# Thirteen instead of eleven tile pairs of an up projection by seven products, eight of them without a full tile between every two

## The chip, the cores and the metric

One core of a Trainium2 chip runs the whole kernel. The metric is the device time of one execution in microseconds (us), the median of several. Below, PE is the matrix engine, DVE the vector engine, ACT the scalar engine, POOL the general one, and SP the queue that issues most loads. POOL issues the loads that add to what is in the buffer already.

## The reference, cut to what matters

A decoder layer for 512 tokens and 1024 channels: three token mixers, an output projection, and then a gated feed-forward part, which the change touches:

```python
h2 = rms_norm(x, norm_ffn[l])                                    # 512 x 1024
up = causal_dwconv(h2 @ w_up[l], ffn_conv_w[l], ffn_conv_b[l])   # w_up 1024 x 6144, width 3
gate_h, val_h = jnp.split(up, 2, axis=-1)                        # 3072 channels each
x = x + (jax.nn.gelu(gate_h, approximate=True) * val_h) @ w_down[l]
```

## The kernel before, in words

The output of the up projection is made in 24 pairs of tiles: pair `i` is 128 gate channels and the 128 value channels that belong to them, each for all 512 tokens. Every float32 factor is split into a high and a low part (`split`, L97 on ACT makes the high part, L98 on DVE the low one), and each product is three matmuls instead of one (`mm3`, L104: high by high, high by low, low by high).

**A full pair** is two units, one for the gate tile and one for the value tile. A unit loads 128x1024 weights into one of three `raw` buffers (L167), splits them into `whi` and `wlo`, and runs 8 x 3 = 24 matmuls with 512 columns. Its result goes through the convolution: one ACT pass (L1184) and two DVE passes, called taps here (L1186). Gate and value meet in a gelu (L1198, ACT) and a product (L1199, DVE).

**A pair by seven products** (`up_fast`) halves the 1024 input channels and the 512 tokens, and needs seven products of half size instead of eight. Each product is 4 x 3 = 12 matmuls with 256 columns, 84 in all. Its weights are blocks of w_up: B11 and B21 (upper and lower half of the input channels) of the gate tile, B12 and B22 of the value tile.

| product | weights | PSUM bank | what reads the bank |
|---|---|---|---|
| a1 | B11 | x | ACT copy (L1290) into the first half of the gate |
| a2 | B21 | its own | DVE addition (L1292) to that half |
| c1 | B11+B12 | c | ACT copy into the second half of the value |
| c2 | B22 | c, on top of c1 | ACT copy into the first half of the value |
| b1 | B11+B12+B22 | x, on top of a1 | DVE subtraction (L1295) from that half |
| b2 | B12+B22 | x, on top of b1 | DVE subtraction from the second half of the value |
| b3 | B11+B12+B22+B21 | x, on top of b2 | ACT copy into the second half of the gate, then taps, gelu, product |

Because a1, b1, b2 and b3 accumulate in one bank, each must have been read before the next begins. The sums of weights are made by POOL in the buffer: after a1's split has read B11, a load that adds brings B12 on top of it (L1273), after c1's split B22, after b1's split B21. So each pair has four plain loads of 256 KB on SP (L1264), four adding loads of 256 KB on POOL, and seven splits of 128x512.

The work is a list of units (a full tile or one product), and what prepares a unit is written so many units ahead:

```python
"a1": [(10, lambda: load("B11")), (5, lambda: ready("a1", "B11", "B12"))],
...
"b1": [(2, lambda: ready("b1", "B11", "B21"))],
"b2": [(10, lambda: load("B12")), (7, lambda: add("B12", "B22")), (1, lambda: ready("b2", "B12"))],
```

So a1's split is written five units ahead of a1, and the load that adds B12 stands behind it. A scheduler then moves instructions a little against each other. All buffers of 128x512 that are not weights of full tiles come from one pool of 51 slots; `whi` and `wlo` have four buffers each.

The order before: pairs 0, 1, 2 are full. Then each of eleven pairs by products is written over two periods, and each period holds one full unit D: `b1' a1 D b2' c1 a2 b3' c2` (the mark is for the pair before). Pairs 5, 8, 11, 14, 17 and 19 give these full units, pairs 20 to 23 follow with the down projection. A small subtraction for the down projection (`down_s3`, L1315, DVE) stands at the end of most periods.

Of the kernel before, what the change touches and what calls it, by code (L numbers as in the profile page):

```python
# [9 lines left out]
F32R = mybir.dt.float32r  # L10
# [8 lines left out]
P = 128  # L19
# [15 lines left out]
NF = FF // P  # L35
# [22 lines left out]
def trunk(ctx: ExitStack, tc: tile.TileContext, x, xT, mem, memT, par, wdecay, wch, wv, wg, wmk,  # L58
# [4 lines left out]
    wpool = pool("wpool", NWB)  # L63
# [8 lines left out]
    def nm(s):  # L72
        uid[0] += 1
        return f"{s}_{uid[0]}"
# [4 lines left out]
    def rslot(shape=(P, S)):  # L79
        return apool.tile(list(shape), F32R, tag="s", name=nm("r"))  # L80
# [121 lines left out]
    HB = D // 2  # L202
# [351 lines left out]
    def proj_in(i, evac):  # L554
        return wch[i], D, lambda w: evac(channel_major(w, KD, lambda k: (hh[:, k, :], hl[:, k, :])))
# [222 lines left out]
    b2 = [u for d in range(KD) for u in branch(2, oc, d)]  # L778
# [423 lines left out]
    def up_units(tiles, keep, early=0):  # L1202

        us = []
        first = []
        for n in range(2 * len(tiles)):
            i, half = tiles[n // 2], n % 2
            if n < early:

                def fn(w, n=n):  # L1210
                    first.append((w, channel_major(w, KD, h2k, 0, S // 2)))
                    if n != 1:
                        norm2_flip(2 + n // 2)
# [40 lines left out]
            return h2["h"][at], h2["l"][at]  # L1254
        return tuple(a[:, k % 2, :] for a in h2s[key, k // 2])

    def up_fast(i, keep):

        src = lambda q: wup[NF * (int(q[2]) - 1) + i][:, HB * (int(q[1]) - 1):HB * int(q[1])]
        raw, w, st = {}, {}, {}  # L1260

        def load(q):
            raw[q] = fslot()
            loads.append(nc.sync.dma_start(raw[q], src(q)))  # L1264

        def ready(key, q, more=None):
            w[key] = rslot(), rslot()
            split(*w[key], raw[q])
            if more:
                add(q, more)  # L1270

        def add(q, more):
            nc.gpsimd.dma_start(raw[q], src(more), accum_op=ALU.add)  # L1273

        def run(key):
            if key == "a1":
                st["x"], st["o"] = bank((P, HT)), (fslot(), fslot())
            elif key in ("a2", "c1"):
                st[key] = sbank((P, HT))
            ps = st["c1" if key[0] == "c" else "a2" if key == "a2" else "x"]  # L1280
            hi, lo = w.pop(key)
            k = range(KD // 2)
            mm3(ps, [(*(a[:, j * P:(j + 1) * P] for a in (hi, lo)), *h2_part(key, j)) for j in k],
                key in ("a1", "a2", "c1"), True, key not in ("a1", "a2", "c1"))
            (g, v), tt = st["o"], nc.vector.tensor_tensor

            one, two = slice(0, HT), slice(HT, S)
            if key in ("a1", "c1", "c2", "b3"):
                o = {"a1": g[:, one], "c1": v[:, two], "c2": v[:, one], "b3": g[:, two]}[key]
                nc.scalar.activation(o, ps, AF.Copy)  # L1290
            elif key == "a2":
                tt(out=g[:, one], in0=g[:, one], in1=ps, op=ALU.add)  # L1292
            else:
                o = v[:, one if key == "b1" else two]
                tt(out=o, in0=o, in1=ps, op=ALU.subtract)  # L1295
            if key == "b3":
                up_mix(*(up_evac(a, NF * half + i) for half, a in enumerate((g, v))), i, keep)

        pre = {
            "a1": [(10, lambda: load("B11")), (5, lambda: ready("a1", "B11", "B12"))],  # L1300
            "a2": [(7, lambda: load("B21")), (3, lambda: ready("a2", "B21"))],
            "c1": [(3, lambda: ready("c1", "B11", "B22"))],
            "c2": [(6, lambda: load("B22")), (3, lambda: ready("c2", "B22"))],
            "b1": [(2, lambda: ready("b1", "B11", "B21"))],
            "b2": [(10, lambda: load("B12")), (7, lambda: add("B12", "B22")), (1, lambda: ready("b2", "B12"))],
            "b3": [(2, lambda: ready("b3", "B11"))],
        }
        return {key: (p, lambda key=key: run(key)) for key, p in pre.items()}

# [107 lines left out]
    us = up_units((0, 1, 2), whole, 3)  # L1417
# [1 line left out]
        us[5], [lambda: h2_ready("c2", 0), lambda: h2_ready("c2", 1)])  # L1419


    us = up_units((5, 8, 11, 14, 17, 19), whole) + up_units(range(20, NF), whole)
    ahead = None
    for i, even in zip((3, 4, 6, 7, 9, 10, 12, 13, 15, 16, 18), (None, 0, 2, None, 4, 6, 8, 10, 12, 14, None)):
        f = up_fast(i, whole)
        run([ahead["b1"]] if ahead else [], [f["a1"]], us.pop(0))
        run([ahead["b2"]] if ahead else [], [f["c1"], f["a2"]], [ahead["b3"]] if ahead else [], [f["c2"]])
        if not ahead:
            run([lambda k=k, p=p: h2_ready(k, p) for k in ("b1", "b2") for p in range(2)])
        if even is not None:  # L1430
            run([lambda i=even: down_s3(i)])
        ahead = f
    run([ahead["b1"]], us.pop(0), [lambda: down_s3(16)], [ahead["b2"]], us.pop(0), [ahead["b3"]], [lambda: down_s3(18)])
    down, n = down_fast(5), 0
    for i, u in enumerate(us):
        run(u, down[5 * i:5 * i + 5 if u is not us[-1] else -4])
# [97 lines left out]
```

## Time and profile before

| what | value |
|---|---|
| median of 3 runs | 918.35 us (917.28 to 918.51) |
| profiled execution | 918.04 us, its span 916.3 us |
| PE busy in the span | 906.1 us (99%) |
| DVE, ACT, POOL busy | 661.6 us (72%), 536.4 us (59%), 145.4 us (16%) |
| full units and products, one after the other | 545 to 738 us of the span |
| mean clock granted to PE | 0.998 |

A row of the timeline or of the chain gives the start in the span, the length, the engine, the line, and how many equal instructions it merges ("x12"). The names say what is written from what: `mm<-h2h,whi` is a matmul of a full unit, `mm<-r,r` or `sm<-h2h,r` one of a product, `r<-f,r` the low part of a split, `wlo<-raw,whi` that of a full unit. In brackets stands how long the engine was idle before, and who ended that. A table by stretches gives the busy time of each engine, the granted clock, the share of time in which the DMA engines worked, and what they moved.

### The profile page before, as it was taken

Reading aid. Unit: us, or ns where it says so; the run is one execution under the profiler, and the core shown is the slowest. Engines: PE = TensorE matmul, PEld = TensorE weight load, DVE = VectorE, ACT = ScalarE, POOL = GpSimd, SP = SyncE. Lnnn points to the kernel's source line nnn. Section 1 sums busy time; section 2 is a strip of 40 time slices with the busy share of each in tenths; the row PEclk is TensorE's granted clock in tenths of the full one; section 3 lists DMA queues with packets and bytes.
Section 4 is the critical chain, followed back from the end, with each engine's and each line's share of the span. In section 5 each row is a group of like instructions: output and inputs, shape, how many; then the busy total and the mean of one; then the engine's idle time right before and its main releaser. Section 6 shows DMA issues by size and latency. Waiting matters only on the chain.

```text
span 916.3 us, 13261 instructions
## 1 busy us (share of the span) xinstructions
PE 906.1 (99%) x4786; PEld 789.1 (86%) x4786; DVE 661.6 (72%) x1194; ACT 536.4 (59%) x935; POOL 145.4 (16%) x188
## 2 busy tenths in 40 slices
PE   9999999999999999999999999999999999999996
PEld 7899888888889998888888898999999988888785
DVE  6996854665679568655867588768777679977665
ACT  7765654685865469475534356656565555555544
POOL 0010000000243330221000000122222221315102
PEclk9999999999999999999999999999999999999999
DMA  7446323213377784331147224776767686779612
GB/s 254 130 141 219 99 82 101 82 49 121 106 175 160 187 198 133 111 101 53 37 152 258 70 79 123 174 188 137 204 141 188 139 194 138 163 201 247 139 46 92
DMA packets 55505, 128.55 MB, mean 140 GB/s; under 512 B 6624, under 2 KB 14480, under 8 KB 55440
## 3 DMA queue, kind: packets, MB, share of 16 engines
q1 hardware_dynamic: 37088, 94.99, 31.5%
q0 software_dynamic: 18208, 32.46, 20.7%
q8 instruction: 37, 0.61, 0.3%
q10 hardware_dynamic: 144, 0.26, 0.1%
q14 instruction: 28, 0.23, 0.1%
HBM read 123.23 MB, written 3.67 MB: 138 GB/s over the span
## 4 chain that ended last, share of the span: by engine, by line
PE 89%; DMA 4%; DVE 3%; ACT 2%; issue 1%; POOL 0%; SPq 0%; POOLq 0%; DVEq 0%; ACTq 0%
PE mm L104 77%; PE sm L104 7%; DMA f<-in_wdown 2%; PE mm L443 2%; DMA f<-in_wv 1%; DVE wlo L98 1%; PE sm L1021 1%; DVE f L399 0%; PE sm L1007 0%; PE sm L1023 0%; DMA raw<-in_wch 0%; PE sm L994 0%; DVE f L565 0%; DVE r L98 0%; PE sm L1162 0%
## 5 line engine op out<-in xcount | busy, mean ns | idle before, releaser
L98 DVE TENSOR_TENSOR wlo<-raw,whi 128x1024 fp32r<-128x1024 f32 (+3 forms) x133 | 146.3, 1105 | 65.9 <-ACT whi L97 36.1
L97 ACT ACTIVATE whi<-raw 128x1024 fp32r<-128x1024 f32 (+3 forms) x133 | 125.6, 953 | 114.7 <-PE mm L104 83.3
L104 PE MATMUL mm<-whi,r 128*128 128x512 f32 (+2 forms) x568 | 168.6, 373 | 0.4 <-DVE r L98 0.4
L104 PEld LDWEIGHTS mm<-whi,r 128*128 128x128 f32 x568 | 105.5, 188 | 16.6 <-DVE r L98 0.8
L97 ACT ACTIVATE r<-f 128x512 fp32r<-128x512 f32 (+3 forms) x184 | 91.9, 542 | 41.1 <-DMA f<-in_wup 37.3
L104 PE MATMUL mm<-hh,whi 128*128 128x512 f32 x288 | 113.2, 393 | 0.0
L104 PE MATMUL mm<-hl,whi 128*128 128x512 f32 x288 | 112.4, 390 | 0.0
L104 PE MATMUL mm<-wlo,r 128*128 128x512 f32 (+2 forms) x284 | 105.7, 372 | 0.5 <-DVE wlo L98 0.5
L98 DVE TENSOR_TENSOR r<-f,r 128x512 fp32r<-128x512 f32 (+3 forms) x184 | 102.3, 586 | 4.0 <-ACT r L97 3.7
L104 PE MATMUL mm<-r,whi 128*128 128x512 f32 (+1 forms) x432 | 94.2, 367 | 0.0
L104 PEld LDWEIGHTS mm<-r,whi 128*128 128x128 f32 x432 | 75.2, 189 | 13.1
L1273 POOL DMA_DIRECT2D f<-in_wup x44 | 38.6, 983 | 283.1 <-DVE r L98 232.6
L104 PE MATMUL mm<-r,r 128*128 128x256 f32 (+2 forms) x456 | 81.6, 329 | 0.0
L97 ACT ACTIVATE whi<-f 128x512 fp32r<-128x512 f32 (+2 forms) x90 | 48.2, 579 | 55.7 <-PE mm L104 41.0
L104 PEld LDWEIGHTS mm<-r,r 128*128 128x128 f32 (+1 forms) x456 | 68.8, 187 | 9.7 <-ACT r L97 0.2
L98 DVE TENSOR_TENSOR wlo<-f,whi 128x512 fp32r<-128x512 f32 (+2 forms) x90 | 53.6, 632 | 31.0 <-ACT whi L97 28.1
L104 PE MATMUL mm<-h2l,whi 128*128 128x512 f32 (+1 forms) x200 | 75.7, 382 | 0.0
L104 PE MATMUL mm<-h2h,whi 128*128 128x512 f32 (+1 forms) x200 | 75.4, 382 | 0.0
L104 PE MATMUL mm<-hh,wlo 128*128 128x512 f32 x288 | 71.5, 390 | 0.0
L104 PEld LDWEIGHTS mm<-hh,wlo 128*128 128x128 f32 x288 | 54.0, 188 | 11.2
L104 PEld LDWEIGHTS mm<-hl,whi 128*128 128x128 f32 x288 | 54.1, 188 | 10.9
L104 PEld LDWEIGHTS mm<-hh,whi 128*128 128x128 f32 x288 | 54.1, 188 | 10.9
(258 smaller groups left out, 1613.6 us busy)
## 6 DMA issues: line engine op xcount, KB each, us to landing
raw<-in_wch SPq DMA_DIRECT2D x39, 512.0 KB, 3.5
raw<-in_wup SPq DMA_DIRECT2D x26, 512.0 KB, 4.4
f<-in_wup SPq DMA_DIRECT2D x44, 256.0 KB, 6.1
f<-in_wup POOLq DMA_DIRECT2D x44, 256.0 KB, 5.7
f<-in_wdown POOLq DMA_DIRECT2D x40, 256.0 KB, 8.2
raw<-in_wbr SPq DMA_DIRECT2D x24, 384.0 KB, 3.1
raw<-in_wdown SPq DMA_DIRECT2D x14, 512.0 KB, 5.1
f<-in_wdown SPq DMA_DIRECT2D x20, 256.0 KB, 5.6
```

The source lines that it names most:

```text
L97: nc.scalar.activation(hi, src, AF.Copy)
L98: return (eng or nc.vector).tensor_tensor(out=lo, in0=src, in1=hi.bitcast(F32), op=ALU.subtract)
L104: nc.tensor.matmul(ps, lhsT=l, rhs=r, start=first and i == 0, stop=last and i == len(seq) - 1, skip_group_check=more)
L443: nc.tensor.matmul(ps[u], lhsT=w(a, u, k), rhs=xs["r"][k][j], start=k == 0 and i < n, stop=k == KD - 1 and i >= len(seq) - n)
L1021: nc.tensor.matmul(ps[:, j, :], lhsT=sT[h][:, t, :], rhs=vt[t][hp][:, j, :], start=True, stop=t == 0)
L1273: nc.gpsimd.dma_start(raw[q], src(more), accum_op=ALU.add)
```

## The change

Pairs 3, 4, 6, 8 to 16 and 18 are now made by seven products (thirteen), and pairs 5, 7, 17, 19 and 20 to 23, beside 0 to 2, are full. The first eight of the thirteen are written over three periods each. One period is now `a1 c1' D? b1'' c2' b2'' a2 b3''`, where one mark is for the pair before and two marks are for the pair before that, and D, a full unit, stands only in four of the ten periods (counted from 0: in 1, 4, 7 and 8). The last five pairs have the order of before: the first of the five begins in period 9, beside the end of the eight and with a full unit between its a1 and its c1; the second has no full unit, and the other three have one each. a1 and b1 of the first eight are prepared earlier (six and five units ahead), b3 later (one unit ahead). The split weights of c1 and c2 move from the pool of 51 slots into the two halves of a `whi` and a `wlo` buffer.

```diff
-    def up_fast(i, keep):
+    def up_fast(i, keep, deep):
...
         def ready(key, q, more=None):
-            w[key] = rslot(), rslot()
+            if key == "c1":
+                st["w"] = [wpool.tile([P, 2, HB], F32R, tag=t, name=nm(t)) for t in ("whi", "wlo")]
+            w[key] = tuple(a[:, int(key[1]) - 1, :] for a in st["w"]) if key[0] == "c" else (rslot(), rslot())
             split(*w[key], raw[q])
...
         pre = {
-            "a1": [(10, lambda: load("B11")), (5, lambda: ready("a1", "B11", "B12"))],
+            "a1": [(11, lambda: load("B11")), (6, lambda: ready("a1", "B11", "B12"))] if deep else
+                  [(10, lambda: load("B11")), (5, lambda: ready("a1", "B11", "B12"))],
             "a2": [(7, lambda: load("B21")), (3, lambda: ready("a2", "B21"))],
             "c1": [(3, lambda: ready("c1", "B11", "B22"))],
             "c2": [(6, lambda: load("B22")), (3, lambda: ready("c2", "B22"))],
-            "b1": [(2, lambda: ready("b1", "B11", "B21"))],
+            "b1": [(5 if deep else 2, lambda: ready("b1", "B11", "B21"))],
             "b2": [(10, lambda: load("B12")), (7, lambda: add("B12", "B22")), (1, lambda: ready("b2", "B12"))],
-            "b3": [(2, lambda: ready("b3", "B11"))],
+            "b3": [(1 if deep else 2, lambda: ready("b3", "B11"))],
         }
...
-    us = up_units((5, 8, 11, 14, 17, 19), whole) + up_units(range(20, NF), whole)
-    ahead = None
-    for i, even in zip((3, 4, 6, 7, 9, 10, 12, 13, 15, 16, 18), (None, 0, 2, None, 4, 6, 8, 10, 12, 14, None)):
-        f = up_fast(i, whole)
-        run([ahead["b1"]] if ahead else [], [f["a1"]], us.pop(0))
-        run([ahead["b2"]] if ahead else [], [f["c1"], f["a2"]], [ahead["b3"]] if ahead else [], [f["c2"]])
...
+    us = up_units((5, 7, 17, 19), whole) + up_units(range(20, NF), whole)
+    nd = 8
+    fast = [up_fast(i, whole, k < nd) for k, i in enumerate((3, 4, 6, 8, 9, 10, 11, 12, 13, 14, 15, 16, 18))]
+    even = {1: 0, 2: 2, 4: 4, 5: 6, 6: 8, 8: 10, 10: 12, 11: 14}
+    part = lambda k, key: [fast[k][key]] if 0 <= k < nd else []
+    for k in range(nd + 2):
+        run(part(k, "a1"), part(k - 1, "c1"))
+        if k in (1, 4, 7, 8):
+            run(us.pop(0))
+        run(part(k - 2, "b1"), part(k - 1, "c2"), part(k - 2, "b2"), part(k, "a2"))
+        if k == nd + 1:
+            run([fast[nd]["a1"]], us.pop(0), [fast[nd]["c1"], fast[nd]["a2"]])
+        run(part(k - 2, "b3"))
...
+    run([fast[nd]["c2"]])
+    for k in range(nd + 1, len(fast)):
+        f, g = fast[k], fast[k - 1]
+        run([g["b1"], f["a1"]], us.pop(0) if k > nd + 1 else [], [g["b2"], f["c1"], f["a2"], g["b3"], f["c2"]])
...
```

On PE, 96 matmuls with 512 columns go and 168 with 256 columns come, over the whole program.

Three places of the order as built. **DVE between the subtraction that reads b1 and the one that reads b2.** Before (line 1295 reads the bank, `r` are splits of products, `wlo` that of a full unit, line 1186 are taps):

```order
L1295 TENSOR_TENSOR f_5997<-f_5997,mm_5995 128x256
L1199 TENSOR_TENSOR f_6125<-f_6125,f_6129 128x512
L98 TENSOR_TENSOR r_6170<-f_5951,r_6169 128x512
L1315 TENSOR_TENSOR f_6125<-f_6125 128x256
L98 TENSOR_TENSOR r_6195<-f_5993,r_6194 128x512
L98 TENSOR_TENSOR r_6199<-f_6110,r_6198 128x512
L98 TENSOR_TENSOR wlo_6885<-raw_6882,whi_6884 128x1024
L1186 SCALAR_TENSOR_TENSOR f_6227<-mm_6202,prm,f_6227 128x511
L1295 TENSOR_TENSOR f_5997<-f_5997,mm_5995 128x256
```

Now, in a period without a full unit (lines 1295 and 1315 have become 1297 and 1318; the rows begin with the taps that follow b3 of the pair before):

```order
L1186 SCALAR_TENSOR_TENSOR f_6110<-f_5653,prm,f_6110 128x510
L1186 SCALAR_TENSOR_TENSOR f_6114<-f_5654,prm,f_6114 128x510
L98 TENSOR_TENSOR r_6140<-f_6036,r_6139 128x512
L1199 TENSOR_TENSOR f_6110<-f_6110,f_6114 128x512
L98 TENSOR_TENSOR r_6161<-f_6081,r_6160 128x512
L1297 TENSOR_TENSOR f_5799<-f_5799,mm_5797 128x256
L98 TENSOR_TENSOR r_6178<-f_5982,r_6177 128x512
L1318 TENSOR_TENSOR f_6110<-f_6110 128x256
L98 TENSOR_TENSOR r_6197<-f_5710,r_6196 128x512
L98 TENSOR_TENSOR r_6218<-f_5544,r_6217 128x512
L1297 TENSOR_TENSOR f_5799<-f_5799,mm_5797 128x256
L98 TENSOR_TENSOR wlo_6357<-f_6036,whi_6356 128x512
```

The full unit's split and taps are gone from between the two subtractions, and what is there belongs to the next products: the split of b2 itself, of the next b1, and of b3.

**PE between b2 and b3 in such a period**, now (`mm_5945` is the shared bank; the first row ends b2, the last begins b3; `sm_6369` is a2, `mm_6415` the next pair's a1). Before, all 24 matmuls of c1 and a2 stood here:

```order
L104 MATMUL mm_5945<-r_5645,r_6323 128x256 x2
L104 MATMUL sm_6369<-h2h,r_6303 128x256
L104 MATMUL sm_6369<-h2l,r_6303 128x256
L104 MATMUL sm_6369<-h2h,r_6303 128x256
L104 MATMUL sm_6369<-h2l,r_6303 128x256
L104 MATMUL sm_6369<-h2h,r_6304 128x256 x4
L104 MATMUL mm_6415<-h2l,r_6284 128x256
L104 MATMUL mm_5945<-h2h,r_6352 128x256
```

Nine matmuls are left between b2 and b3; in the same period 23 stand between b1 and b2 (7 of a1, 12 of c2, 4 of a2).

**ACT around c1's split.** Before (line 1184 opens the convolution, `r_6351` is c1's split, whose buffer has just been added to, line 1198 the gelu, `whi_7066` a full unit):

```order
L1184 ACTIVATE f_6310<-f_5997,prm 128x512
L1290 ACTIVATE f_6180<-sm_6258 128x256
L97 ACTIVATE r_6351<-f_6135 128x512
L1198 ACTIVATE f_6306<-f_6306 128x512
L1290 ACTIVATE f_6361<-mm_6360 128x256
L97 ACTIVATE r_6376<-f_6176 128x512
L97 ACTIVATE r_6380<-f_6291 128x512
L97 ACTIVATE whi_7066<-raw_7064 128x1024
```

Now, for the second of the last five pairs, the one that has no full unit (`whi_6901<-f_6696` is c1's split, `r_6923` the split for b2 of the pair before):

```order
L1184 ACTIVATE f_6882<-f_6417,prm 128x512
L1292 ACTIVATE f_6773<-sm_6824 128x256
L97 ACTIVATE whi_6901<-f_6696 128x512
L97 ACTIVATE r_6923<-f_6726 128x512
L97 ACTIVATE whi_7047<-raw_7045 128x1024
L1198 ACTIVATE f_6878<-f_6878 128x512
L97 ACTIVATE whi_6901<-f_6906 128x512
```

The split of b2 and the gelu now stand behind c1's split, which reads a buffer that is being added to.

More of the change, by code (lines that the diff above doesn't have):

```diff
@@ L1419, in trunk @@
         us[5], [lambda: h2_ready("c2", 0), lambda: h2_ready("c2", 1)])
-    us = up_units((5, 8, 11, 14, 17, 19), whole) + up_units(range(20, NF), whole)
-    ahead = None
-    for i, even in zip((3, 4, 6, 7, 9, 10, 12, 13, 15, 16, 18), (None, 0, 2, None, 4, 6, 8, 10, 12, 14, None)):
-        f = up_fast(i, whole)
-        run([ahead["b1"]] if ahead else [], [f["a1"]], us.pop(0))
-        run([ahead["b2"]] if ahead else [], [f["c1"], f["a2"]], [ahead["b3"]] if ahead else [], [f["c2"]])
-        if not ahead:
-            run([lambda k=k, p=p: h2_ready(k, p) for k in ("b1", "b2") for p in range(2)])
[L1430 to L1433, printed above, removed]
+    us = up_units((5, 7, 17, 19), whole) + up_units(range(20, NF), whole)
[11 more added lines that the diff above has]
+        run(part(k - 2, "b3"))
+        if k == 1:
+            run([lambda k=k, p=p: h2_ready(k, p) for k in ("b1", "b2") for p in range(2)])
+        if k in even:
+            run([lambda i=even[k]: down_s3(i)])
+    run([fast[nd]["c2"]])
+    for k in range(nd + 1, len(fast)):
+        f, g = fast[k], fast[k - 1]
+        run([g["b1"], f["a1"]], us.pop(0) if k > nd + 1 else [], [g["b2"], f["c1"], f["a2"], g["b3"], f["c2"]])
+        if k in (10, 11):
+            run([lambda i=even[k]: down_s3(i)])
+    run([fast[-1]["b1"]], us.pop(0), [lambda: down_s3(16), fast[-1]["b2"], fast[-1]["b3"], lambda: down_s3(18)])
     down, n = down_fast(5), 0
```

## The prediction

> **What bounds the kernel now.** I read the page's totals first, then the chain of work that ended last, then a table by stretches, and then the timelines of the engines in one period.
>
> ```profile
> span 916.3 us, 13261 instructions
> PE 906.1 (99%) x4786; PEld 789.1 (86%) x4786; DVE 661.6 (72%) x1194; ACT 536.4 (59%) x935; POOL 145.4 (16%) x188
> ...
> PE 89%; DMA 4%; DVE 3%; ACT 2%; issue 1%; POOL 0%; SPq 0%; POOLq 0%; DVEq 0%; ACTq 0%
> ```
>
> PE works 99% of the span, and 89% of the chain that sets the end is PE. In the stage of the change nothing else is on it:
>
> ```profile
> 598.03 9.78 PE mm L104 x60
> 607.81 2.88 PE sm L104 x24
> 610.69 1.44 PE mm L104 x12
> 612.13 1.44 PE sm L104 x12
> ...
> core 0: us, PE busy (x) PEld busy (x) DVE busy (x) ACT busy (x) POOL busy (x), PEclk, DMA share, GB/s
> 582.00:598.00 16.00, 15.97 (x112) 14.80 (x111) 11.13 (x19) 10.15 (x20) 2.98 (x5) 1.00 0.86 232
> 644.65:660.19 15.54, 15.54 (x111) 14.58 (x110) 11.82 (x20) 8.94 (x17) 3.89 (x6) 1.00 0.70 162
> ```
>
> The chain's four rows are one period: b1, a1, D and b2 (60 matmuls), c1 and a2 (24), b3, c2. They follow each other without a gap, 15.54 us in all, and the last row of the table says the same of another period: PE 15.54 of 15.54 us at full clock. DVE is busy for 76% of it, the DMA engines for 70%. So here PE's own work sets the time, and the question is what it costs to bring more of it per microsecond to the helpers.
>
> **PE's work.** What a full unit and a product take is read from PE's timeline:
>
> ```profile
> 647.37 0.40 PE L104 MATMUL mm<-h2h,whi 128*128 128x512 f32 x1
> 652.84 1.59 PE L104 MATMUL mm<-r,r 128*128 128x256 f32 x12
> 658.59 1.60 PE L104 MATMUL sm<-r,r 128*128 128x256 f32 x12
> 672.21 0.64 PE L104 MATMUL sm<-h2h,r 128*128 128x256 f32 x4
> ```
>
> A full unit begins at 647.37 and the next product at 652.84: 5.47 us for 24 matmuls, 0.228 each. The chain's 24 matmuls of products take 2.88 us: 1.44 a product, 0.120 a matmul. A full pair is 2 x 5.47 = 10.94 us, a pair by products 7 x 1.44 = 10.08. Two pairs change sides: 4 x 5.47 = 21.88 us go, 20.16 come. PE saves **1.72 us**, and as PE never waited in this stage, no more than that can come from it.
>
> The Trainium skill (TensorE: Matmul & The Clock Gate, "Back-to-back issue gap") gives N/2.4 + 2.5 ns for an isolated matmul of N columns, 215.8 ns for 512 and 109.2 for 256. Estimated from that page, the saving would be 96 x 0.2158 - 168 x 0.1092 = 2.37 us. The rows above have 228 and 120 ns with their weight loads, so the sum goes by these.
>
> **DVE, the next engine.** Its rows show how fast it really starts one instruction after the other:
>
> ```profile
> 650.55 0.69 DVE L1199 TENSOR_TENSOR f<-f,f 128x512 f32<-128x512 f32 x1 [2.93 <-ACT f L1198]
> 653.11 1.23 DVE L98 TENSOR_TENSOR wlo<-raw,whi 128x1024 fp32r<-128x1024 f32 x1
> 654.25 0.75 DVE L1186 SCALAR_TENSOR_TENSOR f<-mm,prm,f 128x511 f32<-128x511 f32 x1
> ...
> 656.50 0.69 DVE L1199 TENSOR_TENSOR f<-f,f 128x512 f32<-128x512 f32 x1
> 657.10 0.69 DVE L98 TENSOR_TENSOR r<-f,r 128x512 fp32r<-128x512 f32 x1
> 657.70 0.42 DVE L1292 TENSOR_TENSOR f<-f,sm 128x256 f32<-128x256 f32 x1
> 658.03 1.29 DVE L98 TENSOR_TENSOR r<-f,r 128x512 fp32r<-128x512 f32 x2
> 660.06 2.78 DVE L1186 SCALAR_TENSOR_TENSOR f<-f,prm,f 128x511 f32<-128x511 f32 x4 [0.73 <-ACT f L1184]
> 662.75 0.42 DVE L1295 TENSOR_TENSOR f<-f,mm 128x256 f32<-128x256 f32 x1
> ...
> 672.89 0.42 DVE L1292 TENSOR_TENSOR f<-f,sm 128x256 f32<-128x256 f32 x1 [0.17 <-PE sm L104]
> ```
>
> From start to start a pass of 512 takes 0.60 us (656.50 to 657.10 to 657.70), one of 256 takes 0.33, four taps 2.69. A pair by products needs seven splits (4.20), three small passes on banks (0.99), four taps (2.69), the product (0.60) and the small subtraction (0.33): 8.81 us. Before, a period had 15.54 us for that and a full unit's 1.14 + 2 x 0.67 + half a product, 2.8 us: DVE could wait for ACT for 2.93 us and nobody noticed. Now a period without D has 10.08 us for 8.81. That fits, but DVE has to be in the right place twice: b2 may not start before DVE has read b1 out of the shared bank, nor b3 before it has read b2.
>
> I lay out the period whose rows stand with the change, with zero where b3 of the pair before ends on PE. PE: a1 0 to 1.44, c1 to 2.88, b1 to 4.32, four of a1 to 4.80, c2 to 6.24, five of a2 to 6.84, b2 to 8.28, nine more to 9.36, b3. DVE's taps start 1.47 after b3 (660.06 against 658.59, where the product after b3 starts). Then: taps to 4.16, split 4.76, product 5.36, split 5.96, reading b1 5.96 to 6.38, split of b2 to 6.98, small subtraction, two splits to 8.42. Reading b2 has to wait for PE: the row at 672.89 starts 0.20 after a2's last matmul (672.21 + 4 x 0.12), so it runs from 8.48 to 8.90. PE wants b2 at 6.84 and b3 at 9.36, so both have 0.46 us to spare. In other periods only five to seven matmuls stand between b2 and b3 (0.60 to 0.84 us) where 0.20 + 0.42 and a start are needed: at most a tenth each. I set **0.1 us** for all of them.
>
> ACT has per pair seven splits, four copies, two convolution passes and a gelu. In its rows below the spacing is 0.52 (650.69 to 651.73 for two), 0.27, 0.72 and 0.52: 3.64 + 1.08 + 1.44 + 0.52 = 6.7 of 10.08 us.
>
> **The loads that add.** Each pair has a chain of three on B11, each waiting for the split before:
>
> ```profile
> 602.47 0.63 ACT L97 ACTIVATE r<-f 128x512 fp32r<-128x512 f32 x1 [3.64 <-DMA f<-in_wup]
> ...
> 650.42 0.36 ACT L1290 ACTIVATE f<-mm 128x256 f32<-128x256 f32 x1
> 650.69 1.14 ACT L97 ACTIVATE r<-f 128x512 fp32r<-128x512 f32 x2
> 651.73 1.05 ACT L97 ACTIVATE whi<-raw 128x1024 fp32r<-128x1024 f32 x1
> ...
> 659.21 1.52 ACT L1184 ACTIVATE f<-f,prm 128x512 f32<-128x512 f32 x2
> 660.64 0.36 ACT L1290 ACTIVATE f<-sm 128x256 f32<-128x256 f32 x1
> ...
> 596.84 1.76 POOL L1273 DMA_DIRECT2D f<-in_wup  x2 [6.04 <-DVE r L98]
> ...
> DMA to landing us min/median/max: 3.9/5.8/8.2
> ```
>
> The add for c1 is issued at 596.84, ACT goes on with c1's split at 602.47, 5.63 us later, and PE takes c1 at 607.81 (the chain's second row): 10.97 us from issue to use, some 4.7 us to spare behind the split. In the eight pairs over three periods the splits of a1 and c1 are 11 units apart, of c1 and b1 six units, and use is three to five units further on; nothing there is nearer than before. The last five pairs keep the leads of before, and the second of them has no D. From the unit at which its a1 is split to its c1 there are six or seven products, 8.64 to 10.08 us, where there were seven and a D, 15.54. From issue to use that leaves 10.97 - 5.5 to 6.9 = 4.1 to 5.5 us, and 5.63 + 0.52 are needed: 0.7 to 2.1 us late. But in DVE's order a1's split follows closely on the taps of the full unit, with nothing of a product between, and counted from there c1 is 0.7 us in time. I take **0.4 us** lost, between these ends (-0.7 costs nothing, 2.1).
>
> By the Trainium skill (DMA: Bandwidth & Descriptors, "Anatomy of one DMA — SWDGE (gpsimd) path") such a load takes about 2.0 us plus its bytes over 436 GB/s, an estimate of 2.6 us for 256 KB. By it nothing would be late here and the loss would be 0.1 us; the 5.63 us of the row decide.
>
> How full the DMA engines get:
>
> ```profile
> q0 software_dynamic: 5184, 9.44, 41.9%
> q1 hardware_dynamic: 6294, 13.55, 27.1%
> ...
> f<-in_wup POOLq DMA_DIRECT2D x36, 256.0 KB, 5.8
> f<-in_wup SPq DMA_DIRECT2D x31, 256.0 KB, 5.9
> raw<-in_wup SPq DMA_DIRECT2D x6, 512.0 KB, 5.8
> f<-in_wdown SPq DMA_DIRECT2D x7, 256.0 KB, 4.0
> raw<-in_wdown SPq DMA_DIRECT2D x2, 512.0 KB, 6.2
> ```
>
> These are the 140 us from 598 to 738. The adds use 41.9% of 140 = 58.7 us for 36, 1.63 us each; the plain loads 37.9 us for 54 times 256 KB, 0.70 us. A pair takes 4 x 1.63 + 4 x 0.70 = 9.3 us of all engines: 92% of a period without D. The stretch 582 to 598 above ran at 0.86 with PE at 15.97 of 16 us, so that much is borne; the step to 0.92 no row shows. Where the adds sit is not moved past other queues: POOL issues eight in two periods, 0.87 us each, and SP's loads come eight in a row instead of four behind each `raw`; these stand a period ahead.
>
> **The sum.** -1.72 + 0.1 + 0.4 = -1.2 us. The profiled execution, 918.04 us (span 916.3 and 1.7 around it), would take 916.8; it lies 0.3 under the median of the three runs, and from that, 918.35, I get **917.1 us**.
>
> **The rivals.**
> - *The whole saving, or a little more.* Nothing is late: 916.6, 0.19% under before, and with the spread of the runs shown (917.28 to 918.51) it can be told as faster. For it: the 0.46 us to spare, and leads that were made longer. If a 256-column matmul took half of a 512-column one, PE would save 96 x 0.228 - 168 x 0.114 = 2.74 us, which gives 915.6; against it stands 0.120 in every period (2 in 100). The Trainium skill's rule above is nearly this case.
> - *The adds come late.* At 92% they take the longest time of the row above, 8.2 us, or more, 3 us longer than I set: the pair without D loses 3.4 us instead of 0.4, and the time is 918.35 - 1.72 + 3.5 = 920.1. For it: ACT already waits 3.64 us in a period; against it: only one place is tight.
> - *DVE becomes the bound* in the five periods without D. If the spacing is as long as the durations in the rows (0.69, 0.42, 2.78), a pair needs 7 x 0.69 + 4 x 0.42 + 2.78 + 0.69 = 9.98 us, reading b1 comes 0.4 us later and what ACT is late adds to it. From 0.46 us on each further microsecond is PE's. It decides from 1.72 / 5 = 0.34 us lost per period on; with 0.8 the time is 918.35 - 1.72 + 4.0 = 920.6, slower. Against it: the spacing is steady in all rows.
> - That the change doesn't do what it says is excluded by the count of matmuls.
>
> **How the numbers follow.** What a measurement of this kernel can tell from no change is about 0.2%, 1.84 us: below 916.5 is faster, above 920.2 slower. Chances: 0.50 for my sum with a loss of 0.2 to 2 us, 0.28 for the whole saving with a spread that brings it under 916.5, 0.12 for late adds (five of the twelve beyond 920.2), 0.10 for DVE. So faster 0.28, same 0.57, slower 0.15. The range 916.2 to 919.9 leaves out 0.15 above and 0.05 below.
>
> **What would show it.** Right: 168 more matmuls of 256 columns at 0.120 us, PE without a wait from its first product to the last but for one of some tenths before c1 of the tenth pair by products; DVE idle between taps and reading b1 nearly gone. Wrong: PE waiting for DVE's L1297 before b2 or b3 in several periods (DVE is the bound); ACT waiting for the adds for over 4 us and PE behind it (the DMA is); a matmul spacing other than 0.120 us; or the down projection's loads taking back what was won, where the chain has shown a wait for its weights.

## The result: ten microseconds slower

The changed kernel takes 928.52 us (median of four runs, 925.04 to 930.08), the kernel before 918.01 on the same chip. The ratio is estimated at 1.0097, 95% interval 1.0075 to 1.012; the quotient of the two medians is a little larger, 1.0114. I had forecast 917.1 us and "the same". The sign, the range and the place of the loss were wrong.

The profiled run of the changed kernel takes 925.04 us. The page's totals and the shares of its chain:

```profile
span 923.3 us, 13467 instructions
PE 908.5 (98%) x4858; PEld 791.6 (86%) x4858; DVE 667.6 (72%) x1210; ACT 542.4 (59%) x953; POOL 151.9 (16%) x196
...
PE 84%; DVE 5%; DMA 4%; issue 4%; ACT 3%; SPq 0%; POOL 0%; POOLq 0%; ACTq 0%; DVEq 0%
```

The share of PE in the chain falls from 89% to 84%. Four stretches of the product stage, and the one that was a period before, in the columns of the earlier table:

```profile
582.00:598.00 16.00, 15.24 (x127) 15.05 (x126) 12.53 (x21) 11.89 (x23) 4.35 (x5) 1.00 0.73 135
598.00:614.00 16.00, 15.97 (x114) 14.92 (x113) 12.59 (x22) 8.99 (x19) 5.21 (x6) 1.00 0.92 226
614.00:630.00 16.00, 14.33 (x113) 13.62 (x112) 10.98 (x19) 8.80 (x17) 2.04 (x3) 1.00 0.59 124
630.00:646.00 16.00, 15.82 (x132) 15.62 (x131) 13.66 (x25) 10.43 (x20) 5.78 (x7) 1.00 0.83 184
644.65:660.19 15.54, 15.54 (x108) 14.44 (x107) 12.15 (x19) 10.00 (x17) 2.97 (x4) 1.00 0.76 169
```

PE loses most, 1.67 of 16 us, where DVE is busy for 69% and the DMA engines for 59%; where they are at 79% and 92%, it loses nothing. So the loss isn't where an engine is full. What PE waited for, and below that what ACT waited for, from 545 to 765 us (total, times, longest), first before, then changed:

```profile
PE mm L104 <- ACT h2h L97: 0.3, 1, 0.3
...
ACT r L97 <- DMA f<-in_wup: 37.3, 12, 5.1
```

```profile
PE mm L104 <- DVE f L1297: 3.5, 3, 1.6
PE sm L104 <- ACT r L97: 0.6, 1, 0.6
PE mm L104 <- ACT r L97: 0.6, 1, 0.6
...
ACT whi L97 <- DMA f<-in_wup: 29.7, 11, 5.6
```

ACT waited 37.3 us for loads that add before, and no matmul behind it was late. Now it waits no more than that, but nearly all of it in splits of c1 and c2 (`whi<-f`; a full unit's would be `whi<-raw`; 2.3 of the 29.7 us are for a plain load), and PE waits for the subtractions of L1297. One place shows the path. ACT, DVE and PE around 616 us of the changed kernel (in brackets the idle time before, and its end's cause):

```profile
610.30 0.62 ACT L1198 ACTIVATE f<-f 128x512 f32<-128x512 f32 x1
616.49 0.63 ACT L97 ACTIVATE whi<-f 128x512 fp32r<-128x512 f32 x1 [5.57 <-DMA f<-in_wup]
617.03 0.76 ACT L1184 ACTIVATE f<-mm,prm 128x512 f32<-128x512 f32 x1
617.69 1.14 ACT L97 ACTIVATE r<-f 128x512 fp32r<-128x512 f32 x2
...
617.15 0.69 DVE L98 TENSOR_TENSOR wlo<-f,whi 128x512 fp32r<-128x512 f32 x1 [4.71 <-ACT whi L97]
617.82 0.75 DVE L1186 SCALAR_TENSOR_TENSOR f<-mm,prm,f 128x511 f32<-128x511 f32 x1
618.49 0.68 DVE L98 TENSOR_TENSOR r<-f,r 128x512 fp32r<-128x512 f32 x1
619.09 0.74 DVE L1186 SCALAR_TENSOR_TENSOR f<-mm,prm,f 128x510 f32<-128x510 f32 x1
619.75 0.41 DVE L1297 TENSOR_TENSOR f<-f,mm 128x256 f32<-128x256 f32 x1
...
614.76 1.60 PE L104 MATMUL mm<-r,r 128*128 128x256 f32 x12
...
618.36 0.39 PE L104 MATMUL sm<-h2h,r 128*128 128x256 f32 x1 [0.57 <-ACT r L97]
620.31 1.18 PE L104 MATMUL mm<-r,r 128*128 128x256 f32 x8 [1.09 <-DVE f L1297]
```

The full unit of this period has ended on PE when b1 starts at 614.76. c1's split stands on ACT directly behind a gelu, and ACT is idle for 5.57 us until its add has landed. Behind it in ACT's row wait the convolution pass of the full unit and two splits; on DVE, idle for 4.71 us, the low part of c1's split, two taps, another low part, and only then the subtraction that reads b1. So PE waits twice: at 618.36 for the split of a2, and at 620.31 for the reading of b1. The weights that ACT waited for are not needed for nearly two periods (they belong to the sixth pair, whose c1 PE starts at 635.85): it is the queue behind them that hurts. The chain of waits follows the same steps back to the add, issued at 611.90:

```profile
611.90 0.01 POOLq L1275
611.91 4.56 DMA f<-in_wup
...
616.49 0.64 ACT whi L97
...
617.15 0.69 DVE wlo L98
...
619.83 0.34 DVE f L1297
...
620.31 1.18 PE mm L104 x8
```

**A measure for all kernels.** From PE's rows I took, from 540 us to the end, by how much each matmul starts later than the normal spacing behind the one before (0.229 us for 512 columns, 0.120 for 256; everything over 0.06 us counts, matmuls that a lower clock slows among them): 1.56 us before, 10.62 changed. 918.04 - 1.72 + (10.62 - 1.56) = 925.4, and the profiled run took 925.04. So PE did save its 1.72 us and lost 9.1 to late starts. The rest of the median's loss, 3.5 us, is in runs with a lower granted clock (last section); what lowered it there is not shown.

### The profile page after: what moved, and what is told of

It reads as the page before. It is cut to its first block, busy times and chain, and to the rows that moved or that the text cites. A ratio compares the mean times of both kernels' runs of the same rounds, so it can differ in the third digit from the quotient of the medians.

```text
span 923.3 us, 13467 instructions
## 1 busy us (share of the span) xinstructions
PE 908.5 (98%) x4858; PEld 791.6 (86%) x4858; DVE 667.6 (72%) x1210; ACT 542.4 (59%) x953; POOL 151.9 (16%) x196
## 4 chain that ended last, share of the span: by engine, by line
PE 84%; DVE 5%; DMA 4%; issue 4%; ACT 3%; SPq 0%; POOL 0%; POOLq 0%; ACTq 0%; DVEq 0%
PE mm L104 74%; PE sm L104 5%; DMA f<-in_wup 3%; PE mm L443 2%; DVE wlo L98 2%; ACT whi L97 1%; PE sm L1021 1%; DVE r L98 1%; DVE f L399 0%; PE sm L1007 0%; PE sm L1023 0%; PE sm L994 0%; DMA raw<-in_wch 0%; DVE f L565 0%; DVE f L1186 0%
## 5 line engine op out<-in xcount | busy, mean ns | idle before, releaser
L98 DVE TENSOR_TENSOR wlo<-raw,whi 128x1024 fp32r<-128x1024 f32 (+3 forms) x129 | 141.3, 1101 | 63.4 <-ACT whi L97 33.5
L97 ACT ACTIVATE whi<-f 128x512 fp32r<-128x512 f32 (+2 forms) x116 | 64.0, 589 | 81.3 <-PE mm L104 35.5
L98 DVE TENSOR_TENSOR wlo<-f,whi 128x512 fp32r<-128x512 f32 (+2 forms) x116 | 71.2, 643 | 40.1 <-ACT whi L97 37.0
L98 DVE TENSOR_TENSOR r<-f,r 128x512 fp32r<-128x512 f32 (+3 forms) x172 | 96.0, 579 | 5.5 <-ACT r L97 5.2
L1275 POOL DMA_DIRECT2D f<-in_wup x52 | 45.2, 911 | 288.0 <-DVE h2l L98 126.6
L97 ACT ACTIVATE r<-f 128x512 fp32r<-128x512 f32 (+3 forms) x172 | 85.4, 535 | 10.4 <-DMA f<-in_wup 5.3
L104 PE MATMUL mm<-r,r 128*128 128x256 f32 (+2 forms) x504 | 89.1, 326 | 2.0 <-DVE f L1297 1.1
L104 PEld LDWEIGHTS mm<-r,r 128*128 128x128 f32 (+1 forms) x504 | 74.4, 187 | 13.3 <-ACT r L97 3.1
L104 PE MATMUL mm<-h2l,whi 128*128 128x512 f32 (+1 forms) x168 | 63.2, 380 | 0.0
L104 PE MATMUL mm<-h2h,whi 128*128 128x512 f32 (+1 forms) x168 | 62.9, 380 | 0.0
```

The costliest lines, as they stand in the source:

```text
L97: nc.scalar.activation(hi, src, AF.Copy)
L98: return (eng or nc.vector).tensor_tensor(out=lo, in0=src, in1=hi.bitcast(F32), op=ALU.subtract)
L104: nc.tensor.matmul(ps, lhsT=l, rhs=r, start=first and i == 0, stop=last and i == len(seq) - 1, skip_group_check=more)
```

## The experiments

Theory 1: a split that waits for a load that adds stands too early in the order of ACT and DVE, and what PE needs is queued behind it. Theory 2: DVE has too much to do. Theory 3: the DMA engines have. In the table, "before" is the kernel before, run beside the changed one on the same chip.

| kernel | median, us | before, us | ratio, 95% interval | profiled run, us | late starts, us |
|---|---|---|---|---|---|
| no loads that add | 917.38 | 917.81 | 0.9994 (0.9985 to 1.0004) | 917.61 | 2.86 |
| c1's split held | 924.45 | 917.81 | 1.0072 (1.0054 to 1.009) | 921.84 | 7.57 |
| end in the old order | 927.02 | 917.81 | 1.0094 (1.0075 to 1.0113) | 927.49 | 12.62 |
| c1, c2 in the pool of 51 | 928.18 | 917.81 | 1.0111 (1.0093 to 1.013) | 927.19 | 12.14 |
| two full units at the end | 931.20 | 918.09 | 1.0126 (1.0109 to 1.0144) | 931.45 | 15.33 |
| held, and two full units | 926.20 | 918.09 | 1.0078 (1.0058 to 1.0099) | 928.91 | 13.55 |
| before, c1 and c2 moved | 919.34 | 918.09 | 1.0012 (1.0002 to 1.0022) | 919.17 | 2.57 |
| one tap less | 920.16 | 918.09 | 1.0016 (1.0005 to 1.0026) | 920.27 | 5.82 |
| held, last b3 late | 920.97 | 918.03 | 1.0026 (1.0008 to 1.0044) | 920.96 | 6.21 |
| held, full unit from period 8 | 924.15 | 918.03 | 1.0062 (1.0047 to 1.0077) | 924.74 | 9.70 |
| held, one tap less | 917.25 | 918.03 | 0.9996 (0.9986 to 1.0005) | 917.54 | 2.92 |
| held, last b3 and last c1s late | 920.82 | 919.01 | 1.0028 (1.0017 to 1.0039) | 920.69 | 6.08 |

**No loads that add**

```diff
         def add(q, more):
-            nc.gpsimd.dma_start(raw[q], src(more), accum_op=ALU.add)
+            pass
```

> The changed kernel without any load that adds; the weights of c1, b1, b2 and b3 are then not sums, and this part of the computation is left out. Instructions of PE, DVE and ACT stay as they are. Theory 1 (a split that waits for a load that adds stands too early in the order of ACT and DVE, and what PE waits for is queued behind it): nothing waits, 917 to 919 us, PE without gaps. Theory 2 (DVE has too much to do in the periods without a full unit): at most 1.5 us better than the changed kernel, 927 us or more. Theory 3 (the DMA engines are too busy): the adds are 70% of a pair's DMA time, so this also goes to 917 to 919; the other kernels of this call tell 1 and 3 apart.

917.38 us: the loss is gone, with all of DVE's work in place. Theory 2 falls as the only cause. The run also gives the bound of the whole change: even with no load to wait for, it is level with the kernel before, since 1.3 of the 1.72 us saved go to small late starts (2.86 against 1.56). Whether the loads cost by the splits that wait for them (theory 1) or by their weight on the DMA engines (theory 3), this run can't tell.

**c1's split held.** `issue_after` keeps the instructions of its block behind another on the same engine.

```diff
+    copies = []
+    HELD = ("c1",)
...
-            split(*w[key], raw[q])
+            with tc.issue_after(copies[-1].ins) if copies and key in HELD else ExitStack():
+                split(*w[key], raw[q])
...
-                nc.scalar.activation(o, ps, AF.Copy)
+                copies.append(nc.scalar.activation(o, ps, AF.Copy))
```

> The changed kernel with the split of c1's weights held on ACT behind the ACT copy that was written before it; the same instructions and loads. Theory 1: the waits of PE in the eight pairs over three periods (about 4 us) and at the tenth pair (0.7) go, those of the last pairs (2.4) and of the end (1.9) stay: 923 to 925 us, ACT's wait for loads that add down from 29.7 us to under 12 between 560 and 745 us. Theory 2 and theory 3: the same load on DVE and on the DMA engines, 927 to 930 us.

As theory 1 expected: 924.45, with the same instructions and loads, so theory 3 falls as the only cause. The two subtractions at the same place, and ACT's waits for adds from 560 to 765 us:

```profile
616.80 0.41 DVE L1301 TENSOR_TENSOR f<-f,mm 128x256 f32<-128x256 f32 x1
...
619.54 0.41 DVE L1301 TENSOR_TENSOR f<-f,mm 128x256 f32<-128x256 f32 x1
```

```profile
ACT whi L97 <- DMA f<-in_wup: 11.5, 4, 4.4
...
ACT r L97 <- DMA f<-in_wup: 8.4, 5, 3.1
```

The first subtraction starts at 616.80 instead of 619.75, and no matmul there is late. ACT's waits in the splits of c1 and c2 fall from 29.7 to 11.5 us, those in the other splits rise from 5.3 to 8.4. At the end of the products PE still waits:

```profile
PE mm L104 <- DVE f L1301: 2.8, 2, 2.6
```

**The end in the old order, and c1 and c2 back in the pool**

```diff
-    run([fast[-1]["b1"]], us.pop(0), [lambda: down_s3(16), fast[-1]["b2"], fast[-1]["b3"], lambda: down_s3(18)])
+    run([fast[-1]["b1"]], [lambda: down_s3(16), fast[-1]["b2"]], us.pop(0), [fast[-1]["b3"], lambda: down_s3(18)])
```

> The changed kernel with the last full unit between b2 and b3 of the last product pair again, as before, instead of ahead of b2. Theory 1: the wait of 1.8 us before that b3 goes and nothing else changes, 926.2 to 927.2 us. Rival (the wait only moves, because the sum that b3 needs is as late as it was): within 0.5 us of the changed kernel's 928.5.

927.02 lies in theory 1's range, yet in the profiled run PE starts the last b3 1.95 us late, against 1.80 in the changed kernel, and b2 of two of the last pairs 0.98 and 2.00 us late, against 0.27 and 0.72. So the rival, within 0.5 us of 928.5, missed the time, but it had the mechanism: the wait only moved. b3's add was issued at 750.88 instead of 748.14, and its split could begin at 758.88 instead of 755.22.

```diff
-            if key == "c1":
-                st["w"] = [wpool.tile([P, 2, HB], F32R, tag=t, name=nm(t)) for t in ("whi", "wlo")]
-            w[key] = tuple(a[:, int(key[1]) - 1, :] for a in st["w"]) if key[0] == "c" else (rslot(), rslot())
+            w[key] = rslot(), rslot()
```

> The changed kernel with the split weights of c1 and c2 in the pool of 51 slots again; everything else stays changed. In its order c1's split no longer stands directly behind a1's split. If the move to the other buffers is what let the split of c1 stand so early (theory 1 with this cause): 922 to 925 us. If the early place comes from the three periods themselves, or the loss is DVE's or the DMA engines' load (theories 2 and 3): 927 to 930 us. If the pool of 51 slots is now too small, loads start later and it is slower than 930.

928.18, no better. c1's split no longer stands behind a1's, yet other splits now stand where they wait for an add, for 20.6 us in all, and PE for them:

```profile
PE mm L104 <- ACT r L97: 3.8, 3, 1.4
PE sm L104 <- ACT r L97: 2.3, 1, 2.3
...
ACT r L97 <- DMA f<-in_wup: 20.6, 9, 4.3
```

So the move of the buffers decides which split stands too early, not that one does. Why the scheduler puts it there stays open.

**Two full units at the end, alone and with c1's split held.** The second comes from pair 20.

```diff
-    run([fast[-1]["b1"]], us.pop(0), [lambda: down_s3(16), fast[-1]["b2"], fast[-1]["b3"], lambda: down_s3(18)])
+    run([fast[-1]["b1"]], us.pop(0), [lambda: down_s3(16), fast[-1]["b2"]], us.pop(0), [fast[-1]["b3"], lambda: down_s3(18)])
```

> The changed kernel with two full units at the end of the products, one between b1 and b2 and one between b2 and b3 of the last product pair, as before (the changed kernel has one, the second comes later then). Theory 1 (the last b3 waits because its split, which waits for a load that adds, stands on DVE ahead of the subtraction that reads b2, and five splits of the down projection behind it): the wait of 1.8 us before b3 is covered, 926 to 927 us. Rival (it only moves, as when the one full unit was put elsewhere): 928 us or more, and the same wait in the trace.

> Both at once: c1's split held on ACT behind the ACT copy written before it, and two full units at the end. Theory 1: of the waits of PE only those of 0.2 to 0.5 us at four places stay, 1.5 us in all, which the saving of 1.72 pays for: 917.5 to 919.5 us, the granted clock back to 0.998. Theory 2 (DVE) and theory 3 (DMA engines too busy) both leave the load as it is: 922 us or more, since with the first hold alone it was 924.45.

Theory 1 missed both times: 931.20 and 926.20 lie in the ranges of its rivals. But the first rival had expected the old wait before b3 in the trace, and that is gone: from 740 to 765 us no matmul starts over 0.41 us late any more. Instead a wait of 2.8 us arose some 120 us later, in the down projection (the row is that of the held kernel):

```profile
881.51 0.76 PE L104 MATMUL mm<-whi,r 128*128 128x512 f32 x1 [2.81 <-DVE m L1362]
```

With one full unit fewer to go beside it, the down projection's work is spread over six units instead of seven. That this shift is what makes DVE late there was only argued.

**The kernel before with the buffers of c1 and c2 moved**

```diff
-            w[key] = rslot(), rslot()
+            if key == "c1":
+                st["w"] = [wpool.tile([P, 2, HB], F32R, tag=t, name=nm(t)) for t in ("whi", "wlo")]
+            w[key] = tuple(a[:, int(key[1]) - 1, :] for a in st["w"]) if key[0] == "c" else (rslot(), rslot())
```

> The kernel before with one part of the change alone: the split weights of c1 and c2 in halves of a whi and a wlo buffer. In its order c1's split stands early too. If an early split costs only where no full unit stands behind it (theory 1): 917 to 919 us, ACT waiting for loads that add longer than before, and PE without a wait. If the move of the buffers is a loss of its own: 920 to 924 us.

919.34, 0.12% over the kernel before and just above the range of theory 1. PE's waits stay at 0.2 us in the trace, so where a full unit stands in each period, the move costs a microsecond, not four or more. That ACT would wait longer was wrong: 13.9 us against 37.3, and 4.4 of the 13.9 are for a plain load. No wait for an add is over 2 us here, so this run doesn't show what a full unit does for an early split that waits as long as the one at 616 us.

**One tap less, then one tap less and c1's split held**

```diff
-    def up_evac(ps, f):
+    def up_evac(ps, f, taps=2):
...
-        for j in (1, 2):
+        for j in (1, 2)[:taps]:
...
-                up_mix(*(up_evac(a, NF * half + i) for half, a in enumerate((g, v))), i, keep)
+                up_mix(*(up_evac(a, NF * half + i, 1) for half, a in enumerate((g, v))), i, keep)
```

> The changed kernel with one tap less in each tile of the product pairs, so two passes of 512 less on DVE per period (1.3 of 8.8 us); this part of the convolution is left out. Theory 2 (DVE's load makes the subtractions late): most of the loss goes, 919 to 922 us. Theory 1 (they stand behind a split that waits for a load): at most 2 us better, 926 to 929 us, the waits of ACT for loads that add still over 20 us.

920.16: a miss for theory 1 alone. ACT waits for adds as long as in the changed kernel, but only half of PE's late starts stay:

```profile
ACT whi L97 <- DMA f<-in_wup: 29.7, 10, 5.7
```

Late starts of over 0.15 us, in us, by place: in the eight pairs (590 to 625 us of the span), and from the last pairs to the end (688 to 765 us):

| kernel | 590 to 625 | 688 to 765 |
|---|---|---|
| changed | 3.3 | 3.6 |
| c1's split held | 0.2 | 3.9 |
| one tap less | 3.1 | 0.2 |
| both | 0.0 | 1.0 |

The hold cures the first place and not the second, less work on DVE the second and not the first. So I split the theory: in the eight pairs the early split of c1 alone is enough; from the last pairs on it takes a late split and a DVE that has no time to catch up. If so, both together must cure both:

> c1's split held, and one tap less in each tile of the product pairs (this part of the convolution is left out). If the early split of c1 and DVE's load are two causes of different waits (the first of those in the eight pairs, the second of those in the last pairs and at the end): both go and it is 916.5 to 918.5 us. If they are one (DVE falls behind wherever it has waited, and either cure is enough): no better than with one tap less alone, 919.5 to 920.5 us.

917.25 us, within 0.15 us of the kernel without adds: two causes, with two cures that add up (late starts of 10.62 us fall by 3.05, by 4.80, and by 7.70 with both).

**The last b3's split late, c1's held.** The trace of the changed kernel at the end shows DVE's queue:

```profile
755.89 0.69 DVE L98 TENSOR_TENSOR r<-f,r 128x512 fp32r<-128x512 f32 x1 [2.01 <-ACT r L97]
756.50 3.09 DVE L98 TENSOR_TENSOR wlo<-f,whi 128x512 fp32r<-128x512 f32 x5
759.51 0.74 DVE L1186 SCALAR_TENSOR_TENSOR f<-mm,prm,f 128x511 f32<-128x511 f32 x1
760.17 0.41 DVE L1297 TENSOR_TENSOR f<-f,mm 128x256 f32<-128x256 f32 x1
```

b3's split waits 2 us for its add, five splits for the down projection and a tap follow, and then the subtraction that reads b2, on which b3 itself depends.

```diff
-            "b3": [(1 if deep else 2, lambda: ready("b3", "B11"))],
+            "b3": [(0 if i == 18 else 1 if deep else 2, lambda: ready("b3", "B11"))],
```

> c1's split held as in the earlier kernel, and the split for the last b3 written behind b2 instead of two units ahead of b3, so that on DVE it no longer stands ahead of the subtraction that reads b2; the full units stay where the changed kernel has them. Theory 1 (the 2.8 us before the last b3 come from that split, which waits for a load that adds): the wait falls to under 0.8 us, 919.5 to 922 us. Theory 2 (the six splits of the down projection ahead of the subtraction are too much for DVE by themselves): the wait stays over 1.5 us, 923 us or more.

920.97, as theory 1 expected. Six splits still stand ahead of the subtraction, but they start without a wait, 5 us earlier, and the subtraction runs at 755.89 instead of 760.17. So before the last b3 too it takes a split that waits; DVE's load alone does not make the loss there:

```profile
751.45 3.86 DVE L98 TENSOR_TENSOR wlo<-f,whi 128x512 fp32r<-128x512 f32 x6
755.23 0.74 DVE L1186 SCALAR_TENSOR_TENSOR f<-mm,prm,f 128x511 f32<-128x511 f32 x1
755.89 0.41 DVE L1301 TENSOR_TENSOR f<-f,mm 128x256 f32<-128x256 f32 x1
```

**The second full unit taken from period 8, c1's held**

```diff
-        if k in (1, 4, 7, 8):
+        if k in (1, 4, 7):
```

(and two full units at the end, as above)

> c1's split held, and two full units at the end, the second taken from period 8 and not from the down projection, whose pace stays. If two full units cover the end (theory 1): the wait before the last b3 goes, and without a cover in period 8 at most 0.8 us comes there, 919.5 to 922 us. If each place without a full unit loses some 2 us (theory 2, DVE has no room): the loss moves from the end to period 8, 923 to 926 us.

924.15: the loss moved, as the second expectation had it. PE starts 2.2 us late at 674 and loses another 2.2 in smaller pieces from 660 to 691, where with c1's split held alone it lost 0.2. So the full unit of period 8 had covered something there; whether waits for adds or DVE's work, this run doesn't tell.

**c1's split later in the last five pairs as well.** With b3 mended, 1.8 us of waits were left from 705 to 728: b2's split stood on ACT behind c1's, which waited 4.91 us for its add.

```diff
-            "c1": [(3, lambda: ready("c1", "B11", "B22"))],
+            "c1": [(3 if deep else 1, lambda: ready("c1", "B11", "B22"))],
```

> The kernel with c1's split held and the last b3's split late, and in the last five pairs c1's split written one unit ahead of c1 instead of three, so that on ACT it stands behind b2's split. Theory 1 (the 1.8 us of waits left in the last pairs are b2's split queued behind c1's split, which waits up to 5.4 us for a load that adds): they go, 918.3 to 919.5 us, and the time is that of the kernel before within 0.2%. If c1 or b1 then come late themselves, the waits move by a product or two and it stays at 920.5 us or more.

920.82, no gain (1.0028 against 1.0026), as the second expectation had it. The waits from 705 to 728 are gone; new late starts stand from 690 to 700, the longest of 1.66 us at 700, in the one period of the last five pairs that has no full unit: c1's split comes later, so the add for b1 is issued later, and b1's split waits for it.

```profile
699.39 0.63 ACT L97 ACTIVATE r<-f 128x512 fp32r<-128x512 f32 x1 [4.67 <-DMA f<-in_wup]
```

No version beat the kernel before. The two that are level with it leave out part of the computation.

## Why the prediction was wrong, point by point

- **PE's saving, 1.72 us: borne out.** Neither kernel that is level shows it as a gain, but in all twelve kernels the late starts account for the profiled time to within 1.4 us, in ten of them to within 0.5, when 1.72 is taken off for the eleven that have the change. 917.54 us with 2.92 of late starts is 918.04 - 1.72 + 1.36 = 917.7.
- **The loads that add: the step that failed.** I wrote that the splits of a1 and c1 are eleven units apart and "nothing there is nearer than before". That counted where the code writes the split. The scheduler had put c1's split much further ahead, in the place above directly behind a1's split of the same buffer and a gelu. So it moved instructions by far more than the "a little" of my description. The rows of DVE that I showed had it: `wlo_6357<-f_6036,whi_6356`, a c1, stands nine rows behind `r_6140<-f_6036,r_6139`, the a1 of the same buffer; I had read there only what stands between the subtractions. For the last five pairs I had even written that b2's split and a gelu stand behind c1's, and left them out of the sum. I priced a late add by the product that it feeds (0.4 us, one tight place). Here the late add cost nothing there, and PE lost what stood behind the waiting split: 3.3 us in the eight pairs (3.1 of it gone when that split alone was held), 3.6 after them.
- **The cover.** The 3.64 us that ACT waited in a period before, I used only in a rival, as a sign for it. It was the sign. Nine of the twelve waits before (35.2 of 37.3 us) fell beside a full unit, and the other three were of 1.1 us at most. The wait shown here ended at 649.37, 3.5 us before the full unit's end (652.84), and DVE had read b1 before it:

```profile
649.37 0.63 ACT L97 ACTIVATE r<-f 128x512 fp32r<-128x512 f32 x1 [3.91 <-DMA f<-in_wup]
...
647.21 0.42 DVE L1295 TENSOR_TENSOR f<-f,mm 128x256 f32<-128x256 f32 x1
```

That the change takes full units away is only part of the answer: the longest wait of the eight pairs, at 616 us, has a full unit beside it as well. But it ends 1.7 us behind that unit (616.49 against 614.76), and the reading of b1, which PE wants next, now stands behind the wait and not ahead of it.
- **DVE: spacing right, layout wrong.** 0.60 and 0.33 us a pass hold (617.15, 617.82, 618.49 and so on). But I laid DVE's passes in a row without any wait of DVE itself, gave 0.46 us to spare and set 0.1 us. After an idle stretch of 4.71 us no such margin helps. Nor was there that much to spare: my layout has 90 matmuls, 10.80 us, in a period of 84, 10.08, and where the changed kernel runs undisturbed (602, 631 and 642 us) DVE ends its reading 0.27 to 0.46 us before b2 and only 0.12 to 0.15 before b3, as close as where PE waited for it (620.16 against 620.31). Even without adds the late starts grow by 1.3 us, where the sum had 0.1. "DVE becomes the bound" at 920.6 had the place (L1297 before b2 and b3) and not the whole cause: with all of DVE's work and no adds it is 917.38, but in the last pairs DVE's load decides what a late split costs.
- **The DMA engines, 92%: their load was not the cause.** In the stretch with 0.92 PE loses 0.03 of 16 us, and the adds took 4.9 us to landing in the middle, less than the 5.8 before:

```profile
f<-in_wup POOLq DMA_DIRECT2D x38, 256.0 KB, 4.9
f<-in_wup SPq DMA_DIRECT2D x34, 256.0 KB, 4.8
```

- **The last pairs "have the order of before".** As written, yes; as built, b2's and the last b3's splits stand behind others that wait. I hadn't looked at the end at all, where the largest wait (1.80 us) came.
- **The tests I named** were good: PE waiting for L1297 before b2 or b3 in several periods, and ACT waiting over 4 us for adds with PE behind it. Both came true, at 616 us in one and the same place, and not as two rivals.

## What to carry to other kernels

Here an engine that waited for a transfer cost what stood behind it in its queue, not what the transfer fed: look in the order as built at the instruction that waits, and at the next three on that engine and on the one fed by it. A long wait is free only as long as it ends before what stands behind it is wanted (37 us were free here); before the order around it is changed, find what the waiting instruction holds up. When a cure only moves a wait, as in five kernels here, the slack is gone, and the bound with the suspected cost removed (917.4 us) says early that nothing is to be won.

## What the runs showed of the hardware

A wait of PE can cost more than its length. The four runs of the changed kernel had granted clocks of 0.998, 0.996, 0.995 and 0.994 and took 925.04, 928.07, 928.97 and 930.08 us; with c1's split held and b3 late, where no wait reaches 1 us, six runs had 0.998 and lay within 1.9 us. That a wait lowered the clock in those runs is not shown: only the profiled runs show single matmuls, and a run of the kernel before, whose profiled run has no late start over 0.6 us, took 923.02 us at 0.996. What can happen, the trace of the kernel held with two full units shows. After PE's wait of 2.81 us, 512-column matmuls start 0.43 us apart instead of 0.228, until 887.60, where the spacing is normal again. 6.09 us go for 14 matmuls that otherwise take 3.2, so the wait cost 2.9 us more than its length:

```profile
882.08 0.63 PE L104 MATMUL mm<-wlo,r 128*128 128x512 f32 x1
882.50 0.63 PE L104 MATMUL mm<-whi,r 128*128 128x512 f32 x1
...
887.60 0.39 PE L104 MATMUL mm<-whi,r 128*128 128x512 f32 x1
```

The table by stretches gives the granted clock there as 0.50:

```profile
881.60:885.00 3.40, 3.40 (x8) 2.69 (x9) 3.40 (x7) 0.00 (x0) 0.00 (x0) 0.50 0.00 0
```

In the kernel with c1's split alone held, a wait of 2.61 us before b3 was followed by full speed:

```profile
757.70:761.00 3.30, 3.30 (x20) 2.98 (x21) 2.12 (x5) 2.23 (x4) 2.34 (x3) 1.00 1.03 154
```

In the kernel with c1 and c2 in the pool of 51, a wait of 2.33 us before 696.29 was followed by 256-column matmuls 0.21 us apart, at a granted clock of 0.52 from 698.0 to 701.4. So the longest and the shortest of these three waits slowed the matmuls behind them, and the one between did not; the length alone does not decide it. The Trainium skill (TensorE: Matmul & The Clock Gate, "Part 1: The HAM clock gate (the "warmup" mystery)") tells of a gate that passes half the clock after an idle window of about 3.4 us, in windows that run free of the kernel, and gives 426.7 ns between 512-column matmuls at that clock. The 0.43 us agree, and windows that run free of the kernel would explain why the length alone does not decide, though no run here shows the windows; that 3.4 us of idle time are needed does not agree with the 2.81 and 2.33 us above.
